# Sums of squares on GpSimd and earlier mix loads at a phase seam of a streaming encoder step

## The chip, the cores and the metric

The kernel runs on one core of a Trainium2 chip. The metric is the device time of one execution in microseconds. The kernel before takes 2540.98 us, the median of three runs (2539.72 to 2542.42).

## The reference, cut to what matters

The computation is one layer of a streaming encoder on 64 rows of a running stream and 16 + 512 rows of a new one (T = 592 tokens), model width 2048. One input projection feeds eight heads of differential attention (group A) and eight heads of latent attention (group B). The outputs of both are concatenated and projected; a SwiGLU network follows.

```python
def project(h, pos, lp):
    z = h @ lp['w_in']
    qd, kd, vd = ...                                     # group A: 3072 columns
    cq = rmsnorm(z[..., OFF_CQ:OFF_CKV], lp['mla_q_norm_g'])       # query latents, 512
    qm = (cq @ lp['mla_w_uq']).reshape(...)              # rope on its last 64 columns
    ckv = rmsnorm(z[..., OFF_CKV:OFF_KR], lp['mla_kv_norm_g'])     # key latents, 256
    krope = rope(z[..., OFF_KR:], pos)                   # shared rotary key, 64
    ...
o_d = rmsnorm(o_d, lp['diff_subln_g']) * (1.0 - lam_init)          # per head of A
mix = jnp.concatenate([o_d.reshape(B, L, D_DIFF), o_m.reshape(B, L, D_MLA)], axis=-1)
x = x + mix @ lp['w_out']
...
```

`rmsnorm` needs the sum of squares of each token's latents. The kernel keeps the tokens along the free dimension, so this sum runs over partitions and over the chunks of 128 latents: four chunks for the queries, two for the keys.

## The kernel before

Every float32 product is done as three TensorE products of a high and a low part. `split` makes these parts: ScalarE copies the high part (L156), VectorE subtracts it for the low part (L153). Three products of one chunk (`h x h`, `l x h`, `h x l`) are called a triple here; each is a pair of matmuls, one for each half of the tokens.

**First phase.** `projections` runs the input projection, head by head, then the latents in the order 4, 5 (keys), 6 (rotary key), 0 to 3 (queries). Each chunk becomes a tile `zs[i]` (named zl) of 128x592 on L618. `diff_attend` is the attention of one head of group A; its last steps norm the head's output `o32` (L567) and store it to device memory, `mspill[h]` (L568, on SyncE's queue).

**Second phase.** Its buffers lie over those of the first. `latents` (L700) makes the norm of the key latents, the rotary key `kr`, the split of both, the split of the query latents (`cqh`, `cql`), and the norm of the queries (`rsq`). Its helper `sum_squares` squares each chunk on ScalarE (L683) and multiplies the square by a matrix of ones on TensorE, which adds over partitions and, in the same accumulator, over chunks. `rope` multiplies by a rotation on TensorE (`pr`), by the sine on VectorE and by the cosine on GpSimd (L696). `latent_rows` writes the latents out. `heads` runs group B; `q_project` is its first use of the query latents, with weights `mh`, `ml`. `mix_out` loads the eight stored heads of group A (L770, seven on GpSimd's queue and one on SyncE's), splits them into `mxh` and `mxl` (L772, L773) and multiplies them by the first half of the output weights, 16 column blocks of eight triples. That product is not urgent until the third phase.

**What sets the order.** TensorE's order is written out by a small model of time: every coroutine has a rank, and the lowest rank that is ready in the model goes next. A `yield` gives the model's estimate of the time until a coroutine goes on.

```python
        first = st.spawn(0, latents())
        rows = st.spawn(1, latent_rows(), [first])
        st.spawn(20, heads(), [first])
        st.spawn(30, mix_out())
```

TensorE keeps that order exactly. The order of the other engines is decided by the scheduler of the framework. Each engine works through its own queue in order, the DMAs that it issues included.

Of the kernel before, what the change touches and what calls it, by code (L numbers as in the profile page):

```python
# [13 lines left out]
AF = mybir.ActivationFunctionType  # L14
# [101 lines left out]
def encoder_step(  # L116
# [22 lines left out]
    def store(dst, src):  # L139
        nc.sync.dma_start(dst, src)  # L140
# [8 lines left out]
    def f32(ap):  # L149
        return ap.bitcast(F32)  # L150
# [142 lines left out]
    def ev(ps, n=TH):  # L293
        return ps[:, :, 0:n]

    def hv(t, n=T):
        return t[:, 0:n].rearrange("p (a b) -> p a b", a=2)
# [16 lines left out]
    with ExitStack() as ph:  # L314
# [7 lines left out]
        def pjt():  # L322
            return pj.tile([P, 2, 512], F32, name="ps", tag="ps")
# [7 lines left out]
        def ztile(name="z"):  # L331
            return az.tile([P, T], F32, name=name, tag="z", bufs=Z_BUFS)
# [182 lines left out]
        def diff_attend(h, kh, kl, vh, vl):  # L515
            bias = ap.tile([P, 528], F32, name="bias")
            load(bias, skewed(h, 127, P, 528))
            G.memset(bias[0:64, 464:528], -BIG)  # L518
            bias5 = ap.tile([NS, P + NS], F32, name="bias5")
            load(bias5, skewed(h, 399, NS, P + NS))  # L520
            yield 3.0

            p5 = ap.tile([NS, P + NS], F32, name="p5")
            for b in range(5):
                ls = ap.tile([P, 2], F32, name="ls", tag="ls", bufs=4)
                es = []
                for c in range(2):
                    yield from st.take("sp")
                    n, W, view, vw = scores(b, sbig(), [qs[h % 2][c]], [(kh, kl)])
                    nm = ap.tile([P, 1], F32, name="nm", tag="nm", bufs=4)  # L530
                    e = ap.tile([P, 528], F32, name="e", tag="e", bufs=3)
                    bt = bias5 if b == 4 else bias[:, 528 - W:528]
                    V.tensor_tensor_reduce(
                        out=vw(e[0:n, 0:W]), in0=view, in1=vw(bt), op0=ALU.add, op1=ALU.min,
                        scale=-1.0, scalar=3e38, accum_out=nm[0:n])
                    S.activation(e[0:n, 0:W], e[0:n, 0:W], AF.Exp, bias=nm[0:n], scale=-1.0,
                                 accum_out=ls[0:n, c:c + 1])
                    es.append(e)
                    st.give("sp", 1.2 + 0.0015 * W)
                    if c == 0:  # L540
                        yield 1.2 + 0.0015 * W
                V.reciprocal(ls[0:n], ls[0:n])
                V.tensor_tensor(ls[0:n], ls[0:n], lamv[0:n], op=ALU.mult)
                V.tensor_scalar(es[1][0:n, 0:W], es[1][0:n, 0:W], ls[0:n, 1:2], None, op0=ALU.mult)
                dst = p5 if b == 4 else pt_b[b][:, NS:NS + W]
                V.scalar_tensor_tensor(dst, es[0][0:n, 0:W], ls[0:n, 0:1], es[1][0:n, 0:W],
                                       op0=ALU.mult, op1=ALU.subtract)
                yield 1.2 + 0.0015 * W
            scored[h]["done"] = True
            yield 2.5  # L550

            o32 = ap.tile([P, TQ], F32, name="o32")
            yield from probabilities_times_values(
                pt_b, p5, [(vh[0:OWN, 0, :], vl[0:OWN, 0, :])] + [(vh[:, 1 + t, :], vl[:, 1 + t, :]) for t in range(4)],
                (vh[:, 5, :], vl[:, 5, :]), ap, tbank, pso, 1.0,
                lambda po, lo_, hi_: S.activation(o32[:, lo_:hi_], po, AF.Copy))
            sq = ap.tile([P, TQ], F32, name="sq")
            S.activation(sq, o32, AF.Square)
            yield 3.5
            yield from st.take("sp")  # L560
            pq = sbig("pq")
            for i in range(2):
                PE.matmul(pq[:, i, 0:QH], ones, sq[:, i * QH:(i + 1) * QH], start=True, stop=True)
            V.tensor_scalar(hv(sq, TQ), ev(pq, QH), 1.0 / P, EPS, op0=ALU.mult, op1=ALU.add)
            r = ap.tile([P, TQ], F32, name="r")
            rsqrt(r, sq)
            V.scalar_tensor_tensor(o32, o32, g08, r, op0=ALU.mult, op1=ALU.mult)  # L567
            store(mspill[h], o32)  # L568
            st.give("sp", 1.7)
            yield 2.0  # L570

# [5 lines left out]
        def projections():  # L577
            for h in range(H):
                ps = ps0 if h == 0 else pjt()
                if h:  # L580
                    yield from project(ps, w_in[:, h * P:(h + 1) * P], xs1)
                if h >= 2:
                    yield [scored[h - 2]]
                z = ztile()
                V.scalar_tensor_tensor(hv(z), ev(ps), DH ** -0.5, hv(rb), op0=ALU.mult, op1=ALU.mult)
                for c in range(2):
                    r = slice(c * DH, (c + 1) * DH)
                    split(qs[h % 2][c][0][r, :], qs[h % 2][c][1][r, :], z[r, :])
# [12 lines left out]
                ps = pjt()  # L601
                yield from project(ps, w_in[:, OFF_V + h * P:OFF_V + (h + 1) * P], xs1)
                if h >= 2:
                    yield [att[h - 2]]
                z = ztile()
                V.tensor_tensor(hv(z), ev(ps), hv(rb), op=ALU.mult)
                vh = ap.tile([P, 6, P], F32R, name="vh", bufs=2)
                vl = ap.tile([P, 6, P], F32R, name="vl", bufs=2)
                nat[2 * h + 1] = st.spawn(0, values(h, z, vh, vl))
                att[h] = st.spawn(1, diff_attend(h, kh, kl, vh, vl),  # L610
                                  [nat[2 * h], nat[2 * h + 1]] + ([att[h - 1]] if h else []))
            for i in (4, 5, 6, 0, 1, 2, 3):
                off = OFF_CQ + i * P
                ps = pjt()
                yield from project(ps, w_in[:, off:off + P] if i < 6 else w_in[:, OFF_KR:OFF_KR + 64], xs1,
                                   dup=(i == 6))
                zs[i] = zl.tile([P, T], F32, name=f"zl{i}")
                V.tensor_tensor(hv(zs[i]), ev(ps), hv(rb), op=ALU.mult)  # L618

        for name in ("sp", "tp", "po"):  # L620
            st.bank(name, 1)
# [4 lines left out]
    with ExitStack() as ph:  # L626
# [50 lines left out]
        rq = [[ap.tile([P, T], F32R, name=f"rq{i}{w}") for w in "hl"] for i in range(2)]  # L677
        kr = pz.tile([P, T], F32, name="kr")

        def sum_squares(pq, tiles):  # L680
            for n, z in enumerate(tiles):
                sq = ztile("sq")
                S.activation(sq, z, AF.Square)  # L683
                yield 1.2
                for i in range(2):
                    PE.matmul(pq[:, i, 0:TH], ones, sq[:, i * TH:(i + 1) * TH],
                              start=(n == 0), stop=(n == len(tiles) - 1))

        def rope(dst, z):
            yield from st.take("sp")  # L690
# [8 lines left out]

        def latents():  # L700

            yield from st.take("ps")
            pq = pjt()
            yield from sum_squares(pq, zs[4:6])
            v = ztile("v")
            V.tensor_scalar(hv(v), ev(pq), 1.0 / KVL, EPS, op0=ALU.mult, op1=ALU.add)
            st.give("ps", 1.5)
            r = ztile("r")
            rsqrt(r, v)

            yield from rope(kr, zs[6])
            for i in range(2):
                z = zs[4 + i]
                V.scalar_tensor_tensor(z, z, gkv[:, i:i + 1], r, op0=ALU.mult, op1=ALU.mult)
                split(ch[:, i, 0:T], cl[:, i, 0:T], z)
            yield from st.take("tp")
            pk = tbank("pkr")
            PE.transpose(pk[:, 0:P], rn.rearrange("p a b -> p (a b)"), ident)
# [14 lines left out]
                split_scaled(cqh[i], cql[i], zs[i], gq[:, i:i + 1])  # L733
            yield from st.take("ps")
            pq = pjt()
            yield from sum_squares(pq, zs[0:4])
            v = ztile("v")
            V.tensor_scalar(hv(v), ev(pq), 1.0 / QL, EPS, op0=ALU.mult, op1=ALU.add)
            rsqrt(rsq, v)
# [26 lines left out]

        def mix_out():

            for h in range(H):
                (G if h < H - 1 else nc.sync).dma_start(f32(mixl[h]), mspill[h])  # L770
            for h in range(H):
                S.activation(mixh[h], f32(mixl[h]), AF.Copy)  # L772
                V.tensor_tensor(mixl[h], f32(mixl[h]), f32(mixh[h]), op=ALU.subtract)  # L773
            for i in range(KC):
                wh, wl = weights(w_out[0:1024, i * P:(i + 1) * P].rearrange("(k p) c -> p k c", p=P), 8, P)
                yield from st.take("ps")
# [688 lines left out]
```

## Time and profile before

| quantity | value |
|---|---|
| median of three runs | 2540.98 us (2539.72 to 2542.42) |
| profiled execution, its own time | 2542.49 us |
| span of that execution | 2540.4 us |
| mean granted clock of TensorE | 0.987 |
| start of the first phase's last products | 567.91 us |
| start of the third phase's first products | 869.69 us |

A profile has for each engine its busy time and the groups of instructions. TensorE is named PE, VectorE DVE, ScalarE ACT, GpSimd POOL and SyncE SP. A row of a timeline has the start in us from the span's start, the duration in us, the engine, the line of the kernel, the operation, the tile that it writes and those that it reads, and the number of instructions in the row. In brackets stands how long the engine was idle before and what ended this. The granted clock is a share of TensorE's full speed.

### The profile page before, as it was taken

The page shows a single profiled execution, that of the slowest core. Times are in us where ns is not written, and L with a number is a line of the kernel's source. Part 1 is how long each engine was busy: PE and PEld are TensorE (multiplying, and loading weights), DVE is VectorE, ACT ScalarE, POOL GpSimd, SP SyncE. Part 2 cuts the span into 40 slices and gives each one's busy share as a digit, 9 for nine tenths or more (in the row PEclk, how much of TensorE's full clock was granted, in tenths as well). Part 3 has the DMA queues.
Part 4 walks back from the last instruction along what each step waited for, and adds up shares of the span by engine and source line. Part 5 has one row for each costly group of instructions (what it writes and reads, how often), then busy time and mean ns, then how long its engine had stood idle before and what let it go on. Part 6 is the DMA issues. An engine that isn't in the chain of part 4 may idle for free. (4 is left out here: it accounts for less than half of the span.)

```text
span 2540.4 us, 44841 instructions
## 1 busy us (share of the span) xinstructions
PE 2444.7 (96%) x17847; PEld 2390.7 (94%) x17847; DVE 1802.2 (71%) x2825; ACT 1106.2 (44%) x2008; POOL 742.3 (29%) x621
## 2 busy tenths in 40 slices
PE   6999999998999999999999999999999899999997
PEld 4999999997999888999999999999999899999997
DVE  5455555556555567877777777777777899999985
ACT  5233333334434344444444444444444544444445
POOL 0000000000000065554544545454453222222236
PEclk9999999998999999999999999999999999999999
DMA  6433323234232444333333433333334743442334
GB/s 200 127 94 94 85 80 84 74 100 142 86 99 76 142 146 142 111 123 108 128 128 119 137 102 121 119 124 133 119 121 134 239 149 100 149 158 91 104 107 149
DMA packets 330115, 307.73 MB, mean 121 GB/s; under 512 B 24707, under 2 KB 298506, under 8 KB 329906
## 3 DMA queue, kind: packets, MB, share of 16 engines
q1 hardware_dynamic: 329346, 302.80, 37.9%
q8 instruction: 140, 2.29, 0.4%
q0 software_dynamic: 560, 2.06, 0.2%
q14 instruction: 69, 0.57, 0.1%
HBM read 250.82 MB, written 56.68 MB: 121 GB/s over the span
## 5 line engine op out<-in xcount | busy, mean ns | idle before, releaser
L1057 PE MATMUL m<-bh,wh 128*128 128x288 f32 x3584 | 968.9, 296 | 9.9 <-ACT wh L156 9.9
L1057 PE MATMUL m<-bl,wh 128*128 128x288 f32 x3584 | 968.5, 295 | 0.0
L1057 PEld LDWEIGHTS m<-bh,wh 128*128 128x128 f32 x3584 | 674.5, 188 | 10.8 <-ACT wh L156 10.6
L1057 PEld LDWEIGHTS m<-bl,wh 128*128 128x128 f32 x3584 | 679.5, 190 | 0.1
L1061 PE MATMUL m<-bh,wl 128*128 128x288 f32 x3584 | 584.3, 298 | 13.6 <-DVE wl L153 11.8
L1061 PEld LDWEIGHTS m<-bh,wl 128*128 128x128 f32 x3584 | 512.6, 189 | 23.8 <-DVE wl L153 23.5
L1026 POOL TENSOR_TENSOR ws<-raw 128x512 f32<-128x512 f32 x256 | 341.8, 1343 | 593.5 <-DVE wl L153 354.4
L156 ACT ACTIVATE wh<-ws 128x512 fp32r<-128x512 f32 (+1 forms) x340 | 288.8, 849 | 443.2 <-PE m L1057 301.9
L153 DVE TENSOR_TENSOR wl<-ws,wh 128x512 fp32r<-128x512 f32 (+1 forms) x340 | 381.2, 1121 | 114.0 <-ACT wh L156 109.5
L153 DVE TENSOR_TENSOR wl<-raw,wh 128x512 fp32r<-128x512 f32 x416 | 404.8, 988 | 27.5 <-ACT wh L156 17.8
L156 ACT ACTIVATE wh<-raw 128x512 fp32r<-128x512 f32 x416 | 249.7, 626 | 300.7 <-PE m L1057 281.5
L108 PE MATMUL ps<-xh,wh 128*128 128x296 f32 x992 | 229.4, 313 | 7.3 <-ACT wh L156 7.3
L108 PE MATMUL ps<-xl,wh 128*128 128x296 f32 x992 | 218.9, 302 | 0.0
L108 PE MATMUL ps<-xh,wl 128*128 128x296 f32 x992 | 218.8, 302 | 0.0
L108 PEld LDWEIGHTS ps<-xh,wh 128*128 128x128 f32 x992 | 163.6, 192 | 11.5 <-ACT wh L156 7.5
L108 PEld LDWEIGHTS ps<-xl,wh 128*128 128x128 f32 x992 | 164.1, 192 | 0.0
L108 PEld LDWEIGHTS ps<-xh,wl 128*128 128x128 f32 x992 | 163.7, 192 | 0.3 <-DVE wl L153 0.3
L153 DVE TENSOR_TENSOR wl<-wr,wh 128x1024 fp32r<-128x1024 f32 (+1 forms) x110 | 117.8, 1071 | 44.7 <-ACT wh L156 42.9
L1026 DVE TENSOR_TENSOR ws<-ws,raw 128x512 f32<-128x512 f32 x128 | 91.3, 714 | 73.2 <-POOL ws L1026 66.1
L1296 DVE TENSOR_TENSOR y<-y,m 128x288 f32<-128x288 f32 x280 | 125.7, 449 | 19.3 <-PE m L1061 17.8
L156 ACT ACTIVATE wh<-wr 128x1024 fp32r<-128x1024 f32 (+1 forms) x110 | 101.9, 929 | 80.1 <-PE ps L108 72.7
L518 POOL MEMSET bias<- 64x64 f32 x8 | 1.3, 159 | 412.9 <-DMA bias<-tsk 412.9
(364 smaller groups left out, 3407.0 us busy)
## 6 DMA issues: line engine op xcount, KB each, us to landing
raw<-in_ffn_w_gate SPq DMA_DIRECT2D x44, 1024.0 KB, 7.7
raw<-in_ffn_w_up SPq DMA_DIRECT2D x44, 1024.0 KB, 5.8
raw<-in_ffn_w_down SPq DMA_DIRECT2D x40, 1024.0 KB, 5.4
wr<-in_w_in SPq DMA_DIRECT2D x60, 512.0 KB, 4.0
actspill<-c SPq DMA_DIRECT2D x44, 288.0 KB, 2.1
sumspill<-c SPq DMA_DIRECT2D x20, 576.0 KB, 2.8
bl<-sumspill SPq DMA_DIRECT2D x80, 144.0 KB, 3.3
bl<-actspill SPq DMA_DIRECT2D x68, 144.0 KB, 4.7
```

The lines of the kernel that those rows point to most:

```text
L108: self.tc.keep_in_program_order(self.pe.matmul(out, lhsT, rhs, start=start, stop=stop))
L153: V.tensor_tensor(lo, src, f32(hi), op=ALU.subtract)
L156: S.activation(hi, src, AF.Copy)
L518: G.memset(bias[0:64, 464:528], -BIG)
L1026: engine.tensor_tensor(w[:, k:k + m, :], pick(xs), pick(ys), op=op)
L1057: PE.matmul(banks[p], wh[:, k, :], x, start=first and new and k == 0 and x is hi, stop=False, skip_group_check=not new)
L1061: PE.matmul(banks[p], wl[:, k, :], hi, start=False, stop=last and k == n - 1, skip_group_check=not new)
L1296: V.tensor_tensor(c, c, banks[p], op=ALU.add)
```

## The change

1. The squares of the latents are multiplied and added on GpSimd, so that one product with the matrix of ones is left for the queries and one for the keys. `sum_squares` goes.
2. The norm of the key latents moves into the first phase: a coroutine `key_latents` starts when both key chunks are projected. `latents` then only splits them.
3. The loads of the eight heads, and the split of seven of them, stand at the head of the second phase. All eight loads are on GpSimd's queue. The split of the last head stands at the start of `latents`.
4. The store of the last head moves from SyncE's queue to GpSimd's.

```diff
-            store(mspill[h], o32)
+            (G if h == H - 1 else nc.sync).dma_start(mspill[h], o32)
...
             for i in (4, 5, 6, 0, 1, 2, 3):
+                if i == 6:
+                    yield [nat[2 * H - 2], nat[2 * H - 1]]
+                    st.spawn(2, key_latents())
...
+        def key_latents():
+            a, b = ztile("ka"), ztile("kb")
+            G.tensor_tensor(a, zs[4], zs[4], op=ALU.mult)
+            G.tensor_tensor(b, zs[5], zs[5], op=ALU.mult)
+            G.tensor_tensor(a, a, b, op=ALU.add)
+            yield 8.0
+            yield from st.take("sp")
+            pq = sbig("pl")
+            for i in range(2):
+                PE.matmul(pq[:, i, 0:TH], ones, a[:, i * TH:(i + 1) * TH], start=True, stop=True)
+            V.tensor_scalar(hv(b), ev(pq), 1.0 / KVL, EPS, op0=ALU.mult, op1=ALU.add)
+            st.give("sp", 1.7)
+            rsqrt(a, b)
+            for i in range(2):
+                V.scalar_tensor_tensor(zs[4 + i], zs[4 + i], gkv[:, i:i + 1], a, op0=ALU.mult, op1=ALU.mult)
...
+        def mix_operand(h):
+            S.activation(mixh[h], f32(mixl[h]), AF.Copy)
+            V.tensor_tensor(mixl[h], f32(mixl[h]), f32(mixh[h]), op=ALU.subtract)
+
+        for h in range(H):
+            G.dma_start(f32(mixl[h]), mspill[h])
+        for h in range(H - 1):
+            mix_operand(h)
+        qsum, qsq = ztile("qsum"), ztile("qsq")
+        G.tensor_tensor(qsum, zs[0], zs[0], op=ALU.mult)
+        for i in range(1, 4):
+            G.tensor_tensor(qsq, zs[i], zs[i], op=ALU.mult)
+            G.tensor_tensor(qsum, qsum, qsq, op=ALU.add)
...
         def latents():
 
-            yield from st.take("ps")
-            pq = pjt()
-            yield from sum_squares(pq, zs[4:6])
-            v = ztile("v")
-            V.tensor_scalar(hv(v), ev(pq), 1.0 / KVL, EPS, op0=ALU.mult, op1=ALU.add)
-            st.give("ps", 1.5)
-            r = ztile("r")
-            rsqrt(r, v)
-
+            mix_operand(H - 1)
             yield from rope(kr, zs[6])
             for i in range(2):
-                z = zs[4 + i]
-                V.scalar_tensor_tensor(z, z, gkv[:, i:i + 1], r, op0=ALU.mult, op1=ALU.mult)
-                split(ch[:, i, 0:T], cl[:, i, 0:T], z)
+                split(ch[:, i, 0:T], cl[:, i, 0:T], zs[4 + i])
...
-            yield from sum_squares(pq, zs[0:4])
+            for i in range(2):
+                PE.matmul(pq[:, i, 0:TH], ones, qsum[:, i * TH:(i + 1) * TH], start=True, stop=True)
...
         def mix_out():
 
-            for h in range(H):
-                (G if h < H - 1 else nc.sync).dma_start(f32(mixl[h]), mspill[h])
-            for h in range(H):
-                S.activation(mixh[h], f32(mixl[h]), AF.Copy)
-                V.tensor_tensor(mixl[h], f32(mixl[h]), f32(mixh[h]), op=ALU.subtract)
```

TensorE's order right behind the last product of the input projection (`ps<-xh,wl`), before. `mxh` and `mxl` are the mix operands, `sq,ones` a sum of squares, `pr` the rotary product, `pkr` the transposes of the cached latents.

```order
L108 MATMUL ps<-xh_107,wl 128x296 x2
L108 MATMUL ps<-mxh_6097,wh 128x288 x2
L108 MATMUL ps<-mxl_6105,wh 128x288 x2
L108 MATMUL ps<-mxh_6097,wl 128x288 x2
L108 MATMUL ps<-mxh_6098,wh 128x288 x2
L108 MATMUL ps<-mxl_6106,wh 128x288 x2
L108 MATMUL ps<-mxh_6098,wl 128x288 x2
L108 MATMUL ps<-sq,ones 128x296 x2
L108 MATMUL ps<-mxh_6099,wh 128x288 x2
```

The same place now; `cqh`, `cql` with `mh`, `ml` are the twelve products of the first `q_project`, of which six are shown. Behind the twelve stands the first mix triple.

```order
L108 MATMUL ps<-xh_107,wl 128x296 x2
L108 MATMUL pr<-zl_5420,rot 128x296 x2
L112 MATMUL pkr<-ident,rn 128x128
L112 MATMUL pkr<-ident,cn 128x128 x2
L108 MATMUL ps<-qsum,ones 128x296 x2
L108 MATMUL ps<-cqh_6135,mh 128x296 x2
L108 MATMUL ps<-cql_6139,mh 128x296 x2
L108 MATMUL ps<-cqh_6135,ml 128x296 x2
L108 MATMUL ps<-cqh_6136,mh 128x296 x2
L108 MATMUL ps<-cql_6140,mh 128x296 x2
L108 MATMUL ps<-cqh_6136,ml 128x296 x2
```

The mix triples moved behind `q_project`: before, fourteen of them and all six sums stand ahead of its first product, now none and one sum.

GpSimd's queue now, from the last of the eight loads to the first rotary product of the queries, `zr`. Ahead of it stand the store of the last head, two squares (`qsum`, `qsq`), a memset and the other seven loads:

```order
L704 DMA mxl_6128<-mspill 128x576
L711 TENSOR_TENSOR qsum<-qsum,qsq 128x592
L720 TENSOR_TENSOR kr<-zl_5420,cos 128x592
L710 TENSOR_TENSOR qsq<-zl_5932 128x592
L743 MEMSET rq0l 64x592
L711 TENSOR_TENSOR qsum<-qsum,qsq 128x592
L741 MEMSET rkl_6132 64x720
L710 TENSOR_TENSOR qsq<-zl_6065 128x592
L743 MEMSET rq1l 64x592
L711 TENSOR_TENSOR qsum<-qsum,qsq 128x592
L720 TENSOR_TENSOR zr<-zq,cos 128x592
```

Before, between the memsets and `zr` stood seven loads, the rotary product `kr` and one memset. The seven products for the query latents joined the queue, two of them ahead of the loads and five behind.

VectorE's queue now, from the middle of the seam on (`v` is the mean square of the query latents, `ml` the low part of the query weights):

```order
L701 TENSOR_TENSOR mxl_6127<-mxl_6127,mxh_6119 128x576
L701 TENSOR_TENSOR mxl_6128<-mxl_6128,mxh_6120 128x576
L153 TENSOR_TENSOR rkl_6131<-kr,rkh_6129 64x592
L742 CAST rq0h<-qmsk 64x592
L153 TENSOR_TENSOR rkl_6132<-kr,rkh_6130 64x592
L153 TENSOR_TENSOR rkl_6132<-pkr,rkh_6130 64x128
L740 CAST rkh_6130<-kmsk 64x720
L153 TENSOR_TENSOR cl<-pkr,ch 128x128
L742 CAST rq1h<-qmsk 64x592
L161 SCALAR_TENSOR_TENSOR cql_6141<-zl_5932,gT,cqh_6137 128x592
L161 SCALAR_TENSOR_TENSOR cql_6142<-zl_6065,gT,cqh_6138 128x592
L753 TENSOR_SCALAR v<-ps 128x592
```

The next row is `ml<-mr,mh`. Before, all four `cql` stand together ahead of the eight `mxl`, and `v` and `ml` stand right behind the masks.

More of the change, by code (lines that the diff above doesn't have):

```diff
@@ L678, in encoder_step @@
         kr = pz.tile([P, T], F32, name="kr")
[L680 to L687, printed above, removed]
+        def mix_operand(h):
[10 more added lines that the diff above has]
+            G.tensor_tensor(qsum, qsum, qsq, op=ALU.add)
         def rope(dst, z):
```

## The prediction

> **What bounds the kernel now.** I read the page's busy shares first, then a table of windows around the seam between the first and second phase, then TensorE's waits from there to the end of the second phase, and last the timelines of TensorE, GpSimd, VectorE and SyncE over the seam. The busy shares:
> ```profile
> PE 2444.7 (96%) x17847; PEld 2390.7 (94%) x17847; DVE 1802.2 (71%) x2825; ACT 1106.2 (44%) x2008; POOL 742.3 (29%) x621
> ```
> TensorE has work for nearly all of the span, so a microsecond that it loses or saves is one of the total, unless another engine takes the bound over. The windows (span of the window, then busy time of each engine, granted clock, DMA share, GB/s) show where it isn't full:
> ```profile
> 500.00:560.00 60.00, 60.00 (x441) 59.15 (x440) 28.47 (x62) 18.80 (x38) 0.77 (x2) 1.00 0.26 75
> 560.00:575.00 15.00, 9.34 (x61) 8.54 (x60) 11.03 (x14) 9.21 (x14) 4.98 (x9) 0.89 0.73 242
> 575.00:590.00 15.00, 10.75 (x55) 9.34 (x55) 11.89 (x21) 6.25 (x13) 1.97 (x2) 0.84 0.65 191
> 590.00:605.00 15.00, 13.46 (x70) 11.52 (x70) 8.75 (x14) 6.96 (x11) 0.00 (x0) 0.81 0.26 81
> 605.00:620.00 15.00, 15.00 (x104) 13.95 (x104) 11.85 (x17) 4.20 (x6) 2.15 (x9) 1.00 0.47 138
> ```
> Before 560 and after 605 TensorE is full; the three windows between are all that the change can win, and what is lost there is passed on whole, since afterwards nothing waits for TensorE to catch up. The waits (releaser: sum, count, longest):
> ```profile
> PE ps L108 <- ACT sq L683: 5.5, 1, 5.5
> PE ps L108 <- ACT mxh L772: 5.3, 1, 5.3
> ```
> and TensorE's timeline (start, length, idle before):
> ```profile
> 567.91 0.43 PE L108 MATMUL ps<-xh,wl 128*128 128x296 f32 x2
> 573.68 0.85 PE L108 MATMUL ps<-mxh,wh 128*128 128x288 f32 x2 [5.34 <-ACT mxh L772]
> 574.85 0.85 PE L108 MATMUL ps<-mxl,wh 128*128 128x288 f32 x2 [0.32 <-DVE mxl L773]
> ...
> 579.73 0.53 PE L108 MATMUL ps<-mxl,wh 128*128 128x288 f32 x2 [0.28 <-DVE mxl L773]
> 580.10 0.43 PE L108 MATMUL ps<-mxh,wl 128*128 128x288 f32 x2
> ...
> 582.16 1.16 PE L108 MATMUL pr<-zl,rot 128*128 128x296 f32 x4
> 583.15 0.27 PE L112 MATMUL pkr<-ident,rn 128*128 128x128 f32 x1
> ...
> 583.40 0.51 PE L108 MATMUL ps<-mxh,wh 128*128 128x288 f32 x2
> ...
> 591.54 2.34 PE L108 MATMUL ps<-sq,ones 128*128 128x296 f32 x4 [5.50 <-ACT sq L683]
> ...
> 596.18 0.65 PE L108 MATMUL ps<-mxh,wh 128*128 128x288 f32 x2
> ...
> 600.55 1.16 PE L108 MATMUL ps<-sq,ones 128*128 128x296 f32 x4
> 601.55 0.38 PE L112 MATMUL pn<-ident,zl 128*80 128x128 f32 x2
> ```
> The last projection ends at 568.34. The idle pieces are 5.34, 0.32, 0.28 and 5.50, together 11.4 us. After each long one TensorE runs slowly. From 573.68 to 580.10 it does eight operand pairs and one sum of squares, 8 x 0.265 + 1.0 = 3.1 us at the later pace (a pair starts 0.26 to 0.27 after another, a sum 1.00, as 600.55 to 601.55 shows), in 6.42 - 0.60 of idle = 5.8: 2.7 lost. From 591.54 to 596.18 it does two sums and three pairs, 2.8, in 4.64: 1.8 lost. The seam loses 11.4 + 4.5 = 15.9 us today.
>
> **The change, part by part.** *Fewer sums on TensorE.* Of six sums of squares four go (the squares are added on GpSimd first) and two stay, one of them now in the first phase: 4 x 1.0 = -4.0 us. The one moved to phase 1 delays its end from 568.34 to 569.35. I give the rest of that chain (two multiplies and an add on GpSimd, five VectorE and two ScalarE steps) no price: GpSimd is nearly idle in the 500 to 560 row, VectorE half so, and TensorE's only wait there is
> ```profile
> PE sp L108 <- DVE nm L533: 5.4, 5, 1.9
> ```
> in five pieces since 200 us. Were the cover gone, one more such piece would cost 0 to 1.9.
>
> *What TensorE finds at the seam.* Today it has mix triples (mxh, mxl) between the sums. Afterwards its order is rot product, transposes, the sum of qsum, and all twelve q_project pairs, and only then the first mix triple. TensorE works strictly in that order, so everything of the mix stands behind the sum and behind cqh, cql and ml. Rot product and transposes end at 569.35 + 1.0 + 0.3 = 570.65; then it waits for GpSimd.
>
> *GpSimd's queue.* Its rows today (the seven loads, one rotary product, memsets):
> ```profile
> 559.23 0.69 POOL L727 MEMSET rkl<- 64x720 f32 x1 [84.30 <-PE ps L108]
> 562.49 3.88 POOL L770 DMA_DIRECT2D mxl<-mspill  x7
> 576.26 1.45 POOL L696 TENSOR_TENSOR kr<-zl,cos 128x592 f32<-128x592 f32 x1 [9.89 <-DMA cos<-c_cos]
> 577.65 0.58 POOL L729 MEMSET rq1l<- 64x592 f32 x1
> 608.75 1.46 POOL L696 TENSOR_TENSOR zr<-zq,cos 128x592 f32<-128x592 f32 x1 [30.52 <-DVE zq L797]
> ```
> and VectorE's (the norm of head 7, the latent splits, the mix splits):
> ```profile
> 566.31 0.82 DVE L567 SCALAR_TENSOR_TENSOR o<-o,gT,r 128x576 f32<-128x576 f32 x1
> 571.05 3.07 DVE L161 SCALAR_TENSOR_TENSOR cql<-zl,gT,cqh 128x592 fp32r<-128x592 f32 x4 [0.62 <-ACT cqh L160]
> 574.04 1.42 DVE L773 TENSOR_TENSOR mxl<-mxl,mxh 128x576 fp32r<-128x576 f32 x2
> ```
> A DMA issue there is 3.88 / 7 = 0.55 us, an elementwise product of this size 1.45. New queue: the store of head 7 needs o, which ends at 567.13 today and 1.0 to 1.5 later now (shift, and key-latent work on VectorE): 568.7. Store 569.3; two squares 2.9, memset 0.7: 572.9; eight load issues 4.4: 577.3; then three adds, two squares and the rotary product, 6 x 1.45, and three memsets, 1.9: qsum is complete at 588. Squares never appear in the trace; the product with cos has the same shape and type, and if a square with one operand read twice took VectorE's 0.77 instead, the four would save 2.7, which I don't expect since both operands are still read.
>
> *VectorE's queue.* After q_project's first two pairs come cqh with ml. Today VectorE made all four cql (3.07) ahead of the mix splits. Now the order is wl, two cl, two cql, the rotary product, eight mix splits of 0.71 to 0.75 mixed with the key rows, masks and the transposed cache, and only then cql of chunks 2 and 3, v and ml. Summed from its rows (0.75 an item of full width, 0.28 for 64x128, 0.5 a mask) that is some 19 us after 570.2, plus waits for loads and ACT copies: ml at 592 to 594 if VectorE runs undisturbed.
>
> *Both at once.* This is the step that decides. Beside the rotary product 608.75 to 610.21 on GpSimd runs
> ```profile
> 608.92 1.84 DVE L153 TENSOR_TENSOR ml<-mr,mh 128x512 fp32r<-128x512 f32 x1
> ```
> and the groups by form give (ns, least/median/most)
> ```profile
> L153 DVE TENSOR_TENSOR ml<-mr,mh x24: 411/683/1843, 585.1 to 839.0; 128x512 fp32r<-128x512 f32 x16, 128x256 fp32r<-128x256 f32 x8
> ...
> L1026 POOL TENSOR_TENSOR ws<-raw x256: 1257/1293/2287, 980.8 to 2443.0; 128x512 f32<-128x512 f32 x128
> L1026 DVE TENSOR_TENSOR ws<-ws,raw x128: 679/693/1745, 982.9 to 2441.1; 128x512 f32<-128x512 f32 x128
> ```
> That ml took 1.84 against a median of 0.68: it ended 0.55 to 0.6 after GpSimd's did, as if it started only then. Both engines' adds of the last two rows stretch by about 1.0 at most, each about a whole instruction of the other. So I take it that a VectorE step with two SBUF inputs and a GpSimd product don't run together. The Trainium skill, page "SBUF — State Buffer", section "SBUF: two separate sides", says the same as a rule: these two share a port pair as an exclusive lock for the whole instruction, and the later one waits; a memset on GpSimd, which reads nothing, wouldn't hold such a VectorE step. The one ml row agrees, and no row of this case tests the memset.
>
> Walking both queues forward with that exclusion, nearly each of GpSimd's eight products meets a VectorE item: GpSimd waits some 3 us in all (0 to 1.1 each; both my estimates from the rows above), VectorE some 8 (six waits of 1.1 to 1.5). qsum ends at 591.1, and TensorE's sum starts at 591.2: idle 591.2 - 570.65 = 20.5. It and three slow pairs take 3.0 where 1.8 would do, 1.2 lost. ml is then ready at 601.3 and the third pair-set waits from 593.7 to 601.3: 7.6 idle. Another slow start loses 1.8, as today. Loss 20.5 + 1.2 + 7.6 + 1.8 = 31.1, against 15.9: +15.2.
>
> *Back at the tail.* Eight mix triples are used later, so more of them stand between the last scores. Today's two gaps there:
> ```profile
> 856.93 0.28 PE L108 MATMUL sp<-kmh,qnh 128*64 128x128 f32 x1 [0.89 <-ACT e L877]
> 860.35 0.66 PE L112 MATMUL tp<-ident,p 128*128 128x128 f32 x4 [2.05 <-DVE pol L153]
> ```
> Four triples now stand ahead of the first, which goes: -0.9. The second gap has none behind its transposes and stays; the bounds are nothing and -2.9.
>
> *The store's and loads' queue.* The store is off SyncE, so rot, cos, sin come 0.3 earlier; nothing needs that. On GpSimd the eighth load reads what that store writes. If it must land first, it holds the issue and all squares behind. Bounds, from issue to landing:
> ```profile
> 567.16 0.34 SPq L140 DMA_DIRECT2D mspill<-o  x1
> ...
> 575.33 0.33 SPq L137 DMA_DIRECT2D qmsk<-c_qmask  x1
> ```
> and from the list of DMA issues (median us to landing)
> ```profile
> mspill<-o SPq DMA_DIRECT2D x16, 288.0 KB, 3.2
> ```
> 3.2 is the median; the last one seems to take until about 575.3, 8.1 us, when loads compete. Issued at 569.3 it lands by 572.5 to 577.4, and the eighth load's turn is 576.8 (577 to 578 with the exclusion): nothing by the first, under 1 by the second. I take nothing, since the store is now ahead of the loads.
>
> **Sum:** +15.2 - 4.0 - 0.9 = +10.3 us. The profiled execution took 2542.49 us (span 2540.4 and 2.1 around it), so it would be 2552.8; the median of the runs is 1.5 below that execution, so 2540.98 + 10.3 = 2551.3 is the prediction. About 0.2%, 5.1 us, can be told from no change here.
>
> **Rivals.** *No exclusion, or a VectorE that is never late (0.16).* qsum at 588, TensorE's first idle 17.4; ml at 593, hardly any second idle (1), slow starts 1 to 3: loss about 21.4, +5.5 - 4.0 - 0.9 = +0.6: 2541.6, not slower. For it: only one ml row and the extremes of the adds show exclusion, and VectorE's waiting items may be spread so that few collide. Against it: the row is clear, and ten or more such items face six products. It decides below a VectorE delay of about 4 us.
>
> *Faster (0.04).* TensorE's first wait would have to end at 582, with six GpSimd products, 8.7 us, done in 5 after loads that end at 577. With squares at VectorE's pace (-2.7 in two places), no exclusion and both tail gaps hidden (-2.9): 2541.6 - 2.7 - 2.0 = 2536.9. Only that squares are not in the trace speaks for it.
>
> *Slower still (0.10).* The store lands late (8.1 us and more under the loads), so the eighth load stops GpSimd's queue and every square behind it: +1 to +4, and memsets that also exclude VectorE: up to +2. 2553 to 2557.
>
> *The change doesn't put the mix first.* It does so for the loads and splits, but by the order TensorE's mix is later than before; that is in the forecast.
>
> **How the numbers follow.** The forecast as worked out has 0.70; its own range, by moving o by 0.6, product time by 0.1 and load landing between 3.4 and 8.3, is 2547.5 to 2554. Slower by over 0.2% is the forecast and the slower rival, 0.80; within 0.2% is the first rival, 0.16; faster 0.04. The range leaves out the lower rivals' 0.2 but reaches to the half-way cases between 2541.6 and 2547.5: 2544 to 2557.
>
> **What would show it.** In the new trace: the sum qsum,ones preceded by some 20 us idle released by GpSimd; ml preceded by a later gap of several us; mix splits of 0.75 now about 2 us each in several cases; GpSimd products near 2; TensorE's mix triples starting after 605. The forecast is wrong if the sum starts before 587, if mxl items keep 0.75, or if the second gap is under 2 us.

## The result, and the profile after

The changed kernel takes 2545.56 us, the median of 22 runs (2542.62 to 2548.59), against 2541.28 for the kernel before in the same runs. The ratio is 1.0014 with a 95% interval of 1.0008 to 1.0020: slower, by 4.3 us in the medians (the ratio, which isn't their quotient, makes it 3.6). The prediction was 2551.3, range 2544 to 2557; the direction and most of the mechanism held, the size was 10.3 where 4.3 came.

The profiled execution took 2543.75 us with a span of 2542.0 us. That is only 1.3 above the profiled execution of before, so the two spans don't show the difference. The seam does. From the start of the last projection product to the first product of the third phase it was 869.69 - 567.91 = 301.8 us and is 874.23 - 568.67 = 305.6, and the first phase ends 0.8 later: +4.5 in all. The 0.8 can't be told from chance: over the fourteen profiled kernels the last projection product starts between 565.53 and 570.84 us, at either end in a kernel without the key norm there. In these two executions the third phase, whose code is unchanged, differed by 2.9 us the other way; over the fourteen it takes 1665.9 to 1674.5. The windows over the seam (length, busy time of each engine, granted clock, DMA share, GB/s):

```profile
560.00:575.00 15.00, 10.78 (x71) 9.68 (x69) 10.81 (x12) 7.15 (x10) 6.53 (x10) 1.00 0.61 188
575.00:590.00 15.00, 1.52 (x3) 1.18 (x4) 12.77 (x13) 6.60 (x13) 13.22 (x12) 0.51 0.70 237
590.00:605.00 15.00, 9.53 (x43) 8.56 (x42) 11.25 (x19) 3.45 (x6) 1.48 (x1) 0.69 0.03 9
605.00:620.00 15.00, 15.00 (x105) 13.84 (x104) 7.77 (x12) 3.21 (x5) 1.06 (x9) 1.00 0.48 143
```

TensorE does 1.5 us of work between 575 and 590, GpSimd 13.2 and VectorE 12.8. TensorE's waits there:

```profile
PE ps L108 <- POOL qsum L711: 16.1, 1, 16.1
PE ps L108 <- DVE ml L153: 6.3, 3, 5.5
```

Its timeline, at the seam and at the end of the second phase:

```profile
568.67 0.43 PE L108 MATMUL ps<-xh,wl 128*128 128x296 f32 x2
569.03 1.24 PE L108 MATMUL pr<-zl,rot 128*128 128x296 f32 x4
571.82 0.30 PE L112 MATMUL pkr<-ident,rn 128*128 128x128 f32 x1 [1.55 <-DMA rn<-in_cache_mla_krope]
...
588.48 2.34 PE L108 MATMUL ps<-qsum,ones 128*128 128x296 f32 x4 [16.14 <-POOL qsum L711]
...
597.28 0.86 PE L108 MATMUL ps<-cqh,ml 128*128 128x296 f32 x2 [5.47 <-DVE ml L153]
...
602.82 0.43 PE L108 MATMUL ps<-mxl,wh 128*128 128x288 f32 x2
...
865.97 0.66 PE L112 MATMUL tp<-ident,p 128*128 128x128 f32 x4 [1.40 <-DVE pol L153]
...
874.23 0.79 PE L189 MATMUL m<-mh,wh 128*128 128x288 f32 x2
```

The two long gaps are the two that the prediction named, in its order: the sum of the query latents from GpSimd, then the low part of the query weights from VectorE. The idle before the scores near 857 is gone, and the one behind `pol` fell from 2.05 to 1.40.

GpSimd's timeline shows what the sum waited for. An add alone is 1.43, a square 1.16 to 1.19; the longer ones lie beside work on VectorE, and their extra time fits a wait for it.

```profile
568.39 0.71 POOL L568 DMA_DIRECT2D mspill<-o  x1 [77.22 <-DVE o L567]
569.13 1.19 POOL L708 TENSOR_TENSOR qsum<-zl 128x592 f32<-128x592 f32 x1
...
572.14 4.36 POOL L704 DMA_DIRECT2D mxl<-mspill  x8
576.56 1.43 POOL L711 TENSOR_TENSOR qsum<-qsum,qsq 128x592 f32<-128x592 f32 x1
...
579.34 1.68 POOL L710 TENSOR_TENSOR qsq<-zl 128x592 f32<-128x592 f32 x1
...
581.74 2.72 POOL L711 TENSOR_TENSOR qsum<-qsum,qsq 128x592 f32<-128x592 f32 x1
...
586.72 1.70 POOL L711 TENSOR_TENSOR qsum<-qsum,qsq 128x592 f32<-128x592 f32 x1
```

VectorE's timeline is the other side: a weight split of 1.23 takes 2.58, a pair of mix splits 3.39 instead of 1.4 to 1.5, a mask copy 2.04 instead of 0.53.

```profile
569.95 2.58 DVE L153 TENSOR_TENSOR wl<-wr,wh 128x1024 fp32r<-128x1024 f32 x1
...
578.25 3.39 DVE L701 TENSOR_TENSOR mxl<-mxl,mxh 128x576 fp32r<-128x576 f32 x2 [2.17 <-ACT mxh L700]
...
583.29 1.78 DVE L701 TENSOR_TENSOR mxl<-mxl,mxh 128x576 fp32r<-128x576 f32 x1
585.11 2.04 DVE L740 CAST rkh<-kmsk 64x720 fp32r<-64x720 f32 x1
587.18 1.86 DVE L701 TENSOR_TENSOR mxl<-mxl,mxh 128x576 fp32r<-128x576 f32 x1
...
596.55 0.67 DVE L153 TENSOR_TENSOR ml<-mr,mh 128x512 fp32r<-128x512 f32 x1
```

### The profile page after: what moved, and what is told of

The parts are those of the page before. It is cut to its first block, busy times and chain, and to the rows that moved or that the text cites. A ratio compares the mean times of both kernels' runs of the same rounds, so it can differ in the third digit from the quotient of the medians.

```text
span 2542.0 us, 44817 instructions
## 1 busy us (share of the span) xinstructions
PE 2437.9 (96%) x17831; PEld 2384.5 (94%) x17831; DVE 1811.8 (71%) x2825; ACT 1104.5 (43%) x2002; POOL 758.5 (30%) x633
## 5 line engine op out<-in xcount | busy, mean ns | idle before, releaser
L1071 PE MATMUL m<-bh,wl 128*128 128x288 f32 x3584 | 584.2, 298 | 12.3 <-DVE wl L153 10.3
L156 ACT ACTIVATE wh<-raw 128x512 fp32r<-128x512 f32 x416 | 249.7, 626 | 303.6 <-PE m L1067 280.8
L108 PEld LDWEIGHTS ps<-xh,wh 128*128 128x128 f32 x992 | 163.3, 192 | 10.3 <-ACT wh L156 6.2
L1214 POOL TENSOR_TENSOR c<-c,rb 128x576 f32<-128x576 f32 x44 | 72.9, 1657 | 167.4 <-ACT c L1213 167.4
```

Source lines behind the costliest of these rows:

```text
L108: self.tc.keep_in_program_order(self.pe.matmul(out, lhsT, rhs, start=start, stop=stop))
L156: S.activation(hi, src, AF.Copy)
L1071: PE.matmul(banks[p], wl[:, k, :], hi, start=False, stop=last and k == n - 1, skip_group_check=not new)
L1214: G.tensor_tensor(g[:, f, :], g[:, f, :], rb2, op=ALU.mult)
```

## The experiments

Each median is set against that of the kernel before, measured along with it. "Seam" is the time between the two starts named above, 301.8 before and 305.6 changed; one execution each. The intervals are 4 to 6 us wide, so two kernels of the table whose medians are less than some 3 us apart can't be told from each other by them.

| kernel | against before, us | ratio, 95% interval | seam, us |
|---|---|---|---|
| the change | +4.3 | 1.0014 (1.0008 to 1.0020) | 305.6 |
| keys_only | -1.2 | 0.9996 (0.9987 to 1.0005) | 300.0 |
| qsum_only | -1.7 | 0.9992 (0.9983 to 1.0001) | 304.1 |
| loads_only | -2.6 | 0.9989 (0.9980 to 0.9998) | 301.7 |
| splits_late | +3.4 | 1.0012 (1.0003 to 1.0020) | 304.5 |
| triples_back | -5.5 | 0.9977 (0.9966 to 0.9987) | 296.2 |
| squares_first | +4.1 | 1.0015 (1.0006 to 1.0025) | 305.4 |
| memsets | -1.5 | 0.9995 (0.9986 to 1.0004) | 299.8 |
| squares_on_vector | +1.4 | 1.0003 (0.9994 to 1.0012) | 303.8 |
| old_sums_no_triples | -3.9 | 0.9985 (0.9976 to 0.9994) | 298.9 |
| triples_back_loads_first | -3.5 | 0.9990 (0.9981 to 0.9999) | 299.1 |
| latents_first_everywhere | +2.3 | 1.0008 (0.9999 to 1.0017) | 303.6 |
| keys_only_no_triples | -11.4 | 0.9961 (0.9949 to 0.9974) | 290.4 |

**The parts, one by one.** First the key norm alone: the lines of `key_latents`, and `latents` without its own key sum.

> The kernel before with only the key latents' norm moved to the first phase (squares on GpSimd there). The theory (the change loses time because TensorE, without mix triples at the seam, waits for GpSimd's sum and for VectorE's queue) expects a gain from this part alone: one sum pair fewer (-1.0 us) and the second wait of before, 5.5 us for the key squares on ScalarE, gone or below 2 us; the first wait 5 to 8 us because the loads now stand behind the memsets. In all 3 to 7 us below before, with the first phase longer by 1.0 us or less. The rival (the key norm's chain disturbs the first phase) expects TensorE waits in the first phase beyond the 5.4 us of before and no gain.

TensorE's longest wait of the seam moved to the mix splits, which VectorE now makes behind the latents; the wait for squares went.

```profile
PE ps L108 <- DVE mxl L781: 8.2, 1, 8.2
```

The gain is below what was expected and can't be told from none. The rival fell: the first phase's wait for `nm` is 5.4 us in five pieces as before, and the phase ended at 568.23.

The query squares alone:

```diff
-            yield from sum_squares(pq, zs[0:4])
+            for i in range(2):
+                PE.matmul(pq[:, i, 0:TH], ones, qsum[:, i * TH:(i + 1) * TH], start=True, stop=True)
```

> The kernel before with only the query squares and their sum on GpSimd, in the second phase; key norm, loads and splits as before. Three sum pairs fewer (-3.0 us). The theory expects the loads, which now stand between the products on GpSimd's queue, to come some 4 to 8 us later and TensorE's first wait to grow from 5.3 to 9 to 12 us, the key squares' wait to stay near 5: 0 to +5 us against before. The rival (GpSimd's products cost nothing while mix triples fill TensorE) expects -3 us.

The waits went to the mix splits. The longest, 7.0, isn't for a load: the copy of the first head on ScalarE ended at 573.2, but VectorE was at its four `cql`, which took 8.71 us beside GpSimd's products instead of 3.07. The later loads do stand between the products.

```profile
PE ps L108 <- DVE mxl L780: 7.0, 1, 7.0
PE ps L108 <- ACT mxh L779: 5.3, 1, 5.3
PE pn L112 <- DVE cl L153: 3.5, 1, 3.5
```

```profile
571.71 8.71 DVE L161 SCALAR_TENSOR_TENSOR cql<-zl,gT,cqh 128x592 fp32r<-128x592 f32 x4
```

The seam is 2.3 longer, but the median is 1.7 shorter, with an interval that reaches 1. The two don't agree, and this stays open.

The loads and the store alone:

```diff
-                (G if h < H - 1 else nc.sync).dma_start(f32(mixl[h]), mspill[h])
+        for h in range(H):
+            G.dma_start(f32(mixl[h]), mspill[h])
+        for h in range(H - 1):
+            mix_operand(h)
```

> The kernel before with only the store of the last head and all eight loads on GpSimd at the head of the second phase and the splits ahead; all sums on ScalarE and TensorE as before. TensorE's order is that of before. The theory expects the loads behind the store, from 569 instead of 562.5, so the first wait grows from 5.3 to 8 to 12 us and the second (5.5) stays or shrinks: +2 to +6 us. The rival (the loads' place doesn't matter, only the products on GpSimd do) expects within 1.5 us of before.

The first wait grew by 3.1, as the theory had it, but the second shrank by 2.0, and the small waits for mix splits went. The theory's loss didn't come. The seam is the same, as the rival has it; the median is 2.6 faster, but its interval reaches from 0.5 to 5.1, so it doesn't rule the rival out.

```profile
PE ps L108 <- ACT mxh L690: 8.4, 1, 8.4
PE ps L108 <- ACT sq L683: 3.5, 1, 3.5
```

So none of the three parts is measurably slower alone. Their medians add up to -5.5 us and their seams to +0.4, where the change has +4.3 and +3.8. By both, the loss is in their combination. In each part alone, mix triples still stand ahead of `q_project`; in the change none does, because the yields that let them in stood in `sum_squares` and went with it. That became the second theory.

**Each wait taken away alone.** First VectorE's order:

```diff
-        for h in range(H - 1):
-            mix_operand(h)
...
-            mix_operand(H - 1)
...
         def mix_out():
+            for h in range(H):
+                mix_operand(h)
```

> The changed kernel with one thing undone: the eight mix splits stand in the mix coroutine again, behind the query latents' splits, while loads, products and key norm stay as changed. The theory expects the second wait of the changed kernel (5.5 us for ml) to go to under 1 us, the first (16.1 us for the sum) to stay within 1.5 us, and the stretch of VectorE's steps to remain: 4 to 7 us below the changed kernel, so -3 to 0 us against before. The rival (the second wait comes from exclusion with GpSimd alone, not from VectorE's order) expects the second wait to stay above 3 us.

The second wait went, as expected, but the total is only 0.9 below the change, not 4 to 7: the next product of the chain, the rotary product of the queries, waited instead, and TensorE's clock was slow behind that wait too.

```profile
PE ps L108 <- POOL qsum L709: 15.6, 1, 15.6
PE pr L108 <- DVE zq L806: 3.0, 1, 3.0
```

Then GpSimd's order, with the product code ahead of the loads:

> The changed kernel with the query squares and adds written ahead of the loads; the scheduler then puts all seven ahead of the fifth load on GpSimd's queue, and the loads end some 6 us later. TensorE's order is unchanged. The theory expects the first wait to fall from 16.1 to 6 to 9 us and the second, for cql or ml behind the later mix splits, to rise from 5.5 to 13 to 17: within 2 us of the changed kernel. The rival (GpSimd's sum alone bounds the seam) expects 6 us or more below the changed kernel.

This came out as the theory had it in total. What GpSimd won, the later loads and the stretched VectorE gave back; the second wait was split, 8.5 for `ml` and 3.9 for the high part `mh` on ScalarE.

```profile
PE ps L108 <- DVE ml L153: 9.4, 3, 8.5
PE ps L108 <- POOL qsum L707: 9.3, 1, 9.3
PE ps L108 <- ACT mh L156: 5.2, 5, 3.9
```

**Do GpSimd's products hold VectorE?**

```diff
-            G.tensor_tensor(qsq, zs[i], zs[i], op=ALU.mult)
-            G.tensor_tensor(qsum, qsum, qsq, op=ALU.add)
+            for n in range(2):
+                G.memset(qsq, 1.0)
+            for n in range(2):
+                G.memset(qsum, 1.0)
```

> The changed kernel with each of the seven products of the query squares replaced by two memsets of the same tile on GpSimd (qsum then holds ones: the query norm is left out). A memset reads no SBUF and two take about 1.2 us, a product 1.17 to 1.43. The theory (VectorE steps with two SBUF inputs wait for a GpSimd product, not for a memset) expects the mix splits on VectorE back at 0.71 to 0.80 us each, but copies of masks beside memsets may still stretch; sum at 583 to 586, ml 5 to 7 us earlier than in the changed kernel: 3 to 6 us below it. The rival (any GpSimd work holds VectorE) expects splits of 1.5 to 2 us still.

VectorE's timeline beside the memsets, and from 581.42 to 582.93 beside the one rotary product that GpSimd kept:

```profile
570.77 1.23 DVE L153 TENSOR_TENSOR wl<-wr,wh 128x1024 fp32r<-128x1024 f32 x1
...
579.57 0.76 DVE L701 TENSOR_TENSOR mxl<-mxl,mxh 128x576 fp32r<-128x576 f32 x1
...
581.76 1.79 DVE L701 TENSOR_TENSOR mxl<-mxl,mxh 128x576 fp32r<-128x576 f32 x1
583.58 1.02 DVE L743 CAST rkh<-kmsk 64x720 fp32r<-64x720 f32 x1
```

A mix split takes 0.76 beside memsets and 1.79 beside the product; a mask copy is stretched from 0.53 to 1.02 even beside a memset. The sum started at 583.5, 5.0 earlier though the first phase ended 0.8 later, and the total is 5.8 below the change. The shorter queue is part of that, so the 5.8 isn't the price of exclusion alone. The rule of the Trainium skill told in the prediction ("SBUF — State Buffer", "SBUF: two separate sides") agrees: two SBUF inputs on VectorE wait only for GpSimd work that reads SBUF, and the same section's other case, a VectorE step in a 2-port mode against any GpSimd work, would fit the mask copy, but no run here shows the mode.

All seven products on VectorE (`V.` for `G.` in the same lines):

> The changed kernel with the seven products on VectorE instead of GpSimd. TensorE's order is unchanged; the scheduler puts the seven products ahead of the mix splits and all four query splits behind them. The theory expects VectorE without stretch (mix splits 0.71 to 0.80), 5.4 us more of its own work, the sum at 576 to 580, but the first query split only at 588 to 592 and the end of q_project at 597 to 600 instead of 602.4: 1 to 5 us below the changed kernel. The rival (no exclusion; GpSimd's help is free) expects 4 us or more above it, since VectorE then carries all.

Mix splits are 0.71 to 0.76 but for the first, 0.99. The total is 2.9 below the change by the medians and 1.8 by the seam, as expected but hardly clear of the noise. The sum came only at 583.2, since the scheduler spread the products between the mix splits.

```profile
PE ps L108 <- DVE qsum L711: 13.4, 1, 13.4
PE ps L108 <- DVE cql L161: 3.7, 1, 3.7
```

`ml` was ready 26.8 us after the start of the last projection product, in the change 28.6. So in these traces 5.4 us more of its own work cost VectorE no more than GpSimd's help did.

**TensorE's order.**

```diff
+            yield 9.0
             yield from st.take("ps")
             pq = pjt()
             for i in range(2):
                 PE.matmul(pq[:, i, 0:TH], ones, qsum...)
```

> The changed kernel with one line added: a yield of 9 in the model of time ahead of the product with qsum, so that thirteen mix triples stand on TensorE ahead of the sum, and all else (GpSimd's products, loads, VectorE's order) as changed. The theory (each part of the change gains a little, and together they lose because the old squares' yields, which gave the mix triples their place at the seam, went with them) expects the 16 us wait to be replaced by waits for the mix splits (8 to 11 us from the transposes on) and some 3 us or less at the sum and ml, and 6 to 11 us below the changed kernel, so 2 to 7 below before. The rival (the time goes into GpSimd's and VectorE's queues and their exclusion, whatever TensorE is given) expects no more than 2 us below the changed kernel, since q_project still ends after 600.

With thirteen triples ahead of the sum the change is worth -5.5 us instead of +4.3, as expected. The sum is not waited for any more; GpSimd's queue and VectorE's stretch are the same (weight split 2.57, mask copy 2.04).

```profile
PE ps L108 <- ACT mxh L700: 5.3, 1, 5.3
PE ps L108 <- DVE mxl L701: 3.0, 2, 2.7
```

The opposite test takes the triples away from the kernel before:

```diff
                 S.activation(sq, z, AF.Square)
-                yield 1.2
+                yield 0.0
```

> The kernel before with one number changed: the yield of 1.2 behind each square on ScalarE is 0, so the model of time gives TensorE all six sums and the first q_project with no mix triple between, as in the changed kernel, while squares stay on ScalarE and the loads where they were. The theory (what TensorE is given at the seam decides, the products on GpSimd are second) expects TensorE idle 14 to 22 us between the last projection and the end of q_project instead of 11.4, some 2 to 3 us won at the end of the second phase, and a total 0 to 5 us above before. The rival (GpSimd's products cause the loss) expects it below before, by the waits for squares (5.5 us) that ScalarE now makes without the mix copies between.

This took the second theory down as it stood. This kernel, without triples, is 3.9 faster than before, and its idle time up to the end of `q_project` is 8.9 us, not 14 to 22. Here ScalarE makes its squares, and VectorE the latents, ahead of most of the mix splits. The profiled execution was the slowest of its eleven (2546.03 us, median 2539.09): the first phase ended 2.9 later than in the one of before and the third took 3.8 longer, while the seam was 2.9 shorter.

```profile
PE ps L108 <- ACT sq L683: 7.7, 3, 5.0
PE pr L108 <- DVE zq L797: 2.2, 1, 2.2
```

Putting the loads first in the kernel with the triples:

> The kernel with the triples back, and the seven products on GpSimd written behind the rotary product, so that the scheduler puts the loads ahead of all of them and no product runs beside the first weight and latent splits. The theory expects the first mix triple 1 to 2 us earlier after the last projection, the 2.6 us weight split on VectorE back at 1.2, and the sum not waited for; the total 1 to 3 us below the kernel with the triples back, 5 to 9 below before. The rival (VectorE's queue of splits bounds the triples, and exclusion only moves later) expects within 1 us of the kernel with the triples back.

No gain: against the kernel with the triples back 2.0 us are lost by the medians, whose intervals overlap, and 2.9 by the seam, more than the rival allowed. The weight split took 1.23 again and the first mix wait fell from 5.3 to 4.6, but products and mix splits met more often: the waits for splits rose from 3.0 to 4.3 us in all, and the sum started at 598.4 instead of 596.5.

**Preparing and using in one order.** The third theory: the change loses because TensorE's order is latents first, while GpSimd, ScalarE and VectorE prepare the mix first.

> The changed kernel with two things together: the query squares written ahead of the loads (as in squares_first) and the mix splits behind the latents (as in splits_late). TensorE's order is that of the changed kernel. The theory now (old_sums_no_triples took the earlier one down: TensorE without triples loses only where GpSimd, ScalarE and VectorE prepare the mix ahead of what TensorE needs first) expects what neither alone gave: sum at 580 to 582, ml by 584 to 587, q_project over by 591 instead of 602.4, a new wait of 1 to 4 us for zq, and 4 to 8 us below the changed kernel, so -4 to 0 against before. The rival (a seam without triples always loses some 25 us, wherever the wait stands) expects within 2 us of the changed kernel again, like each alone.

It missed. It is 2.0 below the change by seam and medians, not 4 to 8, and so within what the rival had. The products ahead of the loads meet VectorE's latent splits (a pair that takes 1.45 to 1.57 otherwise), and ScalarE's `mh` still stands behind four mix copies, two of which wait for late loads:

```profile
574.45 3.76 DVE L153 TENSOR_TENSOR cl<-zl,ch 128x592 fp32r<-128x592 f32 x2
578.13 3.76 DVE L161 SCALAR_TENSOR_TENSOR cql<-zl,gT,cqh 128x592 fp32r<-128x592 f32 x2
```

TensorE's longest waits there:

```profile
PE ps L108 <- POOL qsum L707: 8.9, 1, 8.9
PE ps L108 <- ACT mh L156: 6.3, 5, 4.9
```

Last, TensorE's order of the change but with four sums for one, and the query squares on ScalarE (keys_only with the yield at 0):

> The kernel before with the key norm in the first phase (as in keys_only) and the yield of 1.2 behind the four query squares on ScalarE set to 0. TensorE's order at the seam is then that of the changed kernel but for four sums in place of one, while no product of the query squares runs on GpSimd and loads and mix splits stand behind the latents. The theory expects the sums by 582 and q_project over by 586 to 591, 8 to 14 us of idle at the seam, 2 to 3 us won at the end of the second phase, and 3 to 8 us below before. The rival (TensorE's order without triples is the loss) expects 2 us or more above before.

This is the fastest of all, 11.4 us below before by the median of five runs (9.9 by the ratio) and beyond what was expected. `q_project` ends at 586.3. TensorE's longest waits at the seam:

```profile
PE pr L108 <- DMA rot<-c_rot: 1.8, 1, 1.8
PE ps L108 <- DVE ml L153: 1.8, 2, 1.4
PE ps L108 <- ACT sq L702: 1.1, 1, 1.1
```

With TensorE's order the same but for three more sums and earlier transposes of the latents' rows, the seam takes 15.2 us less than in the change. So that order is not the loss by itself; what it is worth depends on where the squares are made. With GpSimd's products, as in the change, triples ahead of the sum gain 9.8 us (triples_back). With ScalarE's squares the kernels without triples are the faster ones: by 3.9 (old_sums_no_triples against before) and by 10.2 (this kernel against keys_only, from which one yield sets it apart).

In the change TensorE had nothing else while GpSimd made the sum behind eight load issues, and while VectorE made the mix splits, stretched by GpSimd's products, ahead of `ml`. How the 15.2 divide between GpSimd's place in the queue, the exclusion and VectorE's order is not settled. Each alone was taken away and returned 0.2 to 5.8. With the sum ahead of the loads and the mix splits behind the latents together (latents_first_everywhere), only 2.0 came back, and 13.2 us of the seam (303.6 against 290.4) still separate that kernel from the fastest. It has the products on GpSimd, the loads behind them and `mh` behind mix copies; no run takes these apart.

## Why the prediction was right or wrong

*What bounds the kernel.* Right. In eleven of the thirteen kernels the seam's difference and the median's agree within 1.1 us, so what TensorE loses there is passed on. For loads_only (2.5 apart) and qsum_only (4.0) they don't, and one profile each doesn't say why.

*Fewer sums, and the key norm in phase 1.* Five sums fewer stand at the seam, as forecast, and no wait was added in the first phase. It ended 0.76 later, for which 1.0 stood, but that is within the scatter of the first phase, so the 1.0 is neither shown nor refuted.

*The first gap.* Right in kind, mis-sized. Forecast 20.5 us, measured 16.1, with 1.55 ahead of it for a load of the cached keys that I had not seen. A square is 1.16 to 1.19, not 1.45 (four times 0.27 is 1.1), and GpSimd waited 0.5, 1.3 and 0.3 for VectorE, 2.1 where I had 3. The alternative that I wrote down and discarded, a cheaper square, was right in part.

*The second gap.* Right in kind: 5.5 against 7.6. VectorE was stretched by 6.9 (1.35, 1.9, 1.0, 1.5, 1.1 in the rows above) where I had 8, and the memsets showed the reason that I gave. `ml` was ready at 597.2, not 601.3: without the stretch that is 590.3, so VectorE's own queue was some 3 us shorter than the 592 to 594 that I had summed.

*Slow clock.* Too small: 3.0 forecast. After the second gap eleven pairs from 597.28 to 602.82 took 5.5 us where 2.9 would do, 2.6 lost; after the first, the sum and two pairs took 3.3 where 1.5 would do, 1.8 lost. Together 4.4. So the seam lost 23.2 + 4.4 = 27.6 against 15.9: +11.7, where +15.2 stood.

*The tail.* The step that failed by its share: -0.9 forecast, -2.9 measured. The stretch from the last projection product to the third phase grew by 3.8; in it lie +11.7 of losses and -5.0 for five sums fewer, so the rest is 3.8 - 11.7 + 5.0 = -2.9. The wait of 0.89 went and the one behind `pol` lost 0.65. Most of the rest is clock: from that row to the third phase it was 869.69 - 860.35 = 9.3 us and is 874.23 - 865.97 = 8.3. Before, the granted clock was 0.59 from 862.4 to 866; now it is 1.00 from 865.9 to 874.2. I take it that the nine triples that now stand ahead of that row keep TensorE at full speed; no run tests this. I had given -2.9 as the bound and chosen the low end. That the bound and the measurement are the same number is luck: the bound was both gaps gone, and 1.40 of the second stayed.

*The sum.* +10.3 forecast, +4.5 in the two traces and +4.3 in the medians: 3.5 of the difference is the seam, 2.0 the tail, 0.2 the first phase.

*The chances.* I gave 0.80 to slower by over 0.2% and 0.16 to within 0.2%. The measured 0.14% lies in the second, and 2545.56 is nearer to the first rival's 2541.6 than to the forecast's 2551.3. That rival's condition did not hold, though: it needed a VectorE delay of less than about 4 us, and VectorE was stretched by 6.9 and TensorE waited for it. The range held because I had drawn it down to the half-way cases, and in this the result was lucky. Of the signs that I had written down, the sum after 587, the stretched mix splits and the second gap came; mix triples only after 605 did not, since they start at 602.38.

*Rivals.* No exclusion is refuted by VectorE's rows and by the memsets. The store that lands late hardly held: in the kernel with memsets the eighth load waited 0.23 for it, in the change the eight issues ran through in 4.36.

## What to carry to other kernels

Before work is moved ahead of a seam, write down for each engine what it does first there, and look whether the engine that bounds takes things in the same order: with the mix prepared first, using it first on TensorE made the change 9.8 us faster. Agreeing orders are not enough, though: with the latents first on all engines only 2.0 came back as long as GpSimd's products stretched VectorE's steps. When helper steps disappear, look for the pauses in a written-out order that disappear with them; here those were where the filler went in. Three parts of which none is measurably slower alone can lose together, so measure the combination against its parts.

## What the runs showed of the hardware that was not expected

- A GpSimd product that reads one tile twice took 1.16 to 1.19 us at 128x592, one that reads two tiles 1.43 to 1.46.
- GpSimd can win twice in a row: the weight split on VectorE that was ready at 569.95 ended 1.09 us after the second of two GpSimd squares and took 2.58 instead of 1.23, as if it had waited for both.
- A mask copy on VectorE with one input was stretched by a GpSimd memset (0.53 to 1.02), a split with two inputs was not (0.76).
- TensorE's slow pace lasted 5 us of work after a gap of 5.5 us (597.28 to 602.4); the sum and two pairs after the gap of 16.1 did not bring it back: the next 5.5 us gap followed 3.3 us later.
